# A one-core decoder layer: the first FFN's opening in a written order, reversed operand buffers, residual rows loaded a step ahead, and 32-column products in larger groups

## The chip, the cores and the metric

The kernel runs on one core of a Trainium2 chip. The core has five engines with a queue of instructions each: PE (TensorE, matrix products; its weight loads are listed apart as PEld), DVE (VectorE), ACT (ScalarE), POOL (GpSimd) and SP (SyncE, which here mainly issues DMAs). They run side by side and wait for each other through semaphores. The metric is the device time of one execution in microseconds (us), the median of the runs.

## The reference

One layer on 1024 tokens of width 1024, with 16 learned meta tokens in front. D_FF is 2816.

```python
h = concat([zeros(pad), meta, x])
h = h + 0.5 * swiglu(rms_norm(h, ffn1_norm), ffn1_w_in, ffn1_w_out)
u = rms_norm(h, mix_norm) @ w_in
...
o = concat([hgrn2(hq, hf, hi, hg, ...), stick_breaking(sq, sk, sv, ...)])
h = h + o @ w_out
h = h + 0.5 * swiglu(rms_norm(h, ffn2_norm), ffn2_w_in, ffn2_w_out)
return h[:, pad + N_META:, :]

def swiglu(h, w_in, w_out):
    g, u = split(h @ w_in, 2)
    return (silu(g) * u) @ w_out
```

The change touches the first FFN, and the first projection behind it by one weight tile.

## The kernel before

**Products.** All inputs are float32. A product of two float32 matrices is made of three matmuls on rounded parts: a number is cast to a high part (`hi`, `wh`) and its remainder (`lo`, `wl`) is kept, and hi·hi, lo·hi and hi·lo are added up in PSUM. The cast is ACT's, the remainder is DVE's. `halve` (L306) does it for the activations, `operand` (L356) for a weight block.

**Halves.** The FFN's two matrix products are block products of 2 by 2 halves that use seven half-size products in place of eight (Strassen's scheme in Winograd's form). For `fast_in` (L348, activations times `w_in`) the right operands are called B11, B21, T2, T3, T1, T4 and B22: B11, B21 and B22 are quarters of the normed, transposed tokens (512 features by 512 tokens each), the T's are sums and differences of them. The left operands are quarters of a weight column block (a11, a21, a22, a12) and sums of them (`s1`, `s2` and others), which POOL makes from loaded `raw` tiles (`made`, L382). One product of this kind, "a group" below, is `times` (L424): 12 matmuls of 128x128 by 128x512.

**A quad.** `quad` (L434) is a generator that makes one pair of column blocks: seven groups in turn, their weights taken one by one from `weights`. Results are added up over PSUM banks "qa", "qb", "qc" and kept copies (`p1`, `u2`, `u3`), and pass through `gate` (L498: SiLU on ACT) or `up` (L507: product on DVE), and the activations go to DRAM by DMAs that POOL issues (L514). `pair` joins the gate's quad and the up quad of the same columns.

**The opening.** PE can start before all operands exist: four pairs (eight quads) are opened by their first two groups, B11 and B21, 16 groups in all; then come the second groups by T2, and so on. Before the first group, `open_tokens` (L708) loads the first four 128-token rows, norms them (`norm_rows`, L679: sum of squares on ACT or DVE in turns, root on ACT, reciprocal and scale on DVE), turns them by 32 PE transposes (`turned`, L698) and makes B11's and B21's hi (L741) and lo (L744). The second four rows and the meta tokens follow while the opener groups run: b22 (L758), the combinations for T2 and T3 (L762, L763), the meta columns (L768), the T2 difference (L777) and its halves, and, spread over the steps, the halves of T3, T1, T4 (after a difference, L783) and B22. `setup_rest` (L101) makes constants for later stages: among them seven mask levels, each a memset on DVE (L114), four affine selects on POOL (L119, L123) and a copy on DVE (L127), all in one buffer `sd`, and two sigmoids on ACT (L135, L136). A scheduler orders the instructions of each engine by priorities; the program hands `fast_in` a `taken` hook that notes the last instruction of an engine in `marks`, and `issue_after` keeps an instruction behind a noted one.

**Residual rows.** `turn_x` (L827) is a generator with a step for each half of a 128-token row: load `xrow` (one buffer) by SP, four transposes (L837), a copy, a DMA to DRAM. `between` takes two steps after each opened pair.

**The second half.** `fast_out` (L569) multiplies the activations by `w_out` in the same scheme: `raw` blocks in a ring of six buffers (L587), seven steps (A11, S1, ..., A12, S3, A22), 11 q steps in each, 12 matmuls a q (L656). The meta tokens are 32 columns wide (`actm`): `meta` (near L1686) puts their small matmuls (`meta_block`, L1676 to L1678) between the q steps.

**The projection behind it.** A pool of weight tiles "we" holds two column tiles of `w_in` loaded during the FFN (`early_w`: key, value, query) for `project_early`; `sb_project` (L1114) loads column 2048 again in its first pass (L1131, as hi and lo halves, through `col_tile`, L237).

Of the kernel before, what the change touches and what calls it, by code (L numbers as in the profile page):

```python
# [20 lines left out]
P = 128  # L21
D = 1024
# [18 lines left out]
class Block:  # L41
# [59 lines left out]
    def setup_rest(self):  # L101
# [33 lines left out]
        nc.scalar.activation(self.lb, mx, AF.Sigmoid)  # L135
        nc.scalar.activation(self.lbc, mx, AF.Sigmoid, scale=-1.0)  # L136
# [211 lines left out]
    def fast_in(self, ops, n, w_in, actD, openers, ev0, open_ev, feed=None, meta=None, spare=None,  # L348
# [84 lines left out]
        def quad(col, take, opened=None, turns=0, keep=None):  # L433
# [3 lines left out]
            def go(bank, op, start):  # L437
                if start:
                    ps[bank] = pin.tile([P, n], F32, tag="q" + bank, name="q" + bank, bufs=2)
                left = ready.pop() if ready else next(w)  # L440
                if op not in made_yet:
                    next(feed)
                    made_yet.add(op)
                times(ps[bank], left, ops[op], start)
                return ps[bank]

            def first():
# [4 lines left out]
                nc.scalar.copy(p1, p)  # L452
                return p1

            def kept(name, x, y):
# [113 lines left out]
    def fast_out(self, hT, cs, n, w_out, actD, ready, between=lambda a, q: None,  # L569
# [37 lines left out]
        def left(step, q):  # L607
# [71 lines left out]
    def norm_rows(self, rows, at, junk):  # L679

        nc = self.nc
        for i, (row, m) in enumerate(rows, at):
            s, r = self.ss[:m, i, 0:1], self.ss[:m, i, 1:2]
            if i % 2:
                nc.vector.scalar_tensor_tensor(
                    junk[1][:m], row[:m], 1.0, row[:m], ALU.mult, ALU.mult, accum_out=s
                )
            else:
                nc.scalar.activation(junk[0][:m], row[:m], AF.Square, accum_out=s)
            self.root = nc.scalar.activation(  # L690
                r, s, AF.Sqrt, bias=self.eps[:m], scale=1.0 / D
            )
            nc.vector.reciprocal(r, r)
            nc.vector.tensor_scalar_mul(row[:m], row[:m], r)

    def turned(self, rows, ks, banks):
# [4 lines left out]
        for i, (row, _) in enumerate(rows):  # L701
# [6 lines left out]
    def open_tokens(self, ops, steps, rows_at, pool, operands):  # L708
# [7 lines left out]
        junk = [rp.tile([P, D], (BF16, U8)[i], name=f"junk{i}") for i in range(2)]  # L716

        def rows_in(r0):
            got = []
            for i in range(4):  # L720
                row = rp.tile([P, D], F32, tag="row", name="row", bufs=8)
                nc.sync.dma_start(row, x[r0 + i * P : r0 + i * P + P])
                got.append((row, P))
# [6 lines left out]
        rows = rows_in(0)  # L730
        kept = {}

        def spare(k):
            nc.scalar.mul((b11 + b21)[k], kept[k], g[k])

        with self.tc.high_priority():
            self.norm_rows(rows, 0, junk)
            kept.update(self.turned(rows, range(KT), "aabbccdd"))
            for k in range(KT):
                hi, lo = (t[:, k % 4, :] for t in ops[("B11", "B21")[k // 4]])  # L740
                nc.scalar.mul(hi, kept[k], g[k])  # L741
                if k == 0:
                    spare(0)
                stt(lo, kept[k], g[k], hi.bitcast(F32), ALU.mult, ALU.subtract)  # L744
        with self.tc.issue_after(self.root.ins):
# [21 lines left out]
        for k in range(KT):  # L767
# [3 lines left out]
        nc.vector.tensor_mul(  # L771
            self.xm[:, :, :META], ps, self.g1.unsqueeze(2).broadcast_to([P, KT, META])
        )
        rows_at.close()
        operands()
        for j in range(4):
            sub(t2[j], b22[j], b11[j])  # L777
            self.halve(ops["T2"], t2[j], j)
        next(steps)
        for o, b in (("T3", t3), ("T1", b11), ("T4", b21), ("B22", b22)):  # L780
# [4 lines left out]
            next(steps)  # L785

    def meta_in(self):
# [7 lines left out]
        def finish():  # L795
# [3 lines left out]
            if col < D_FF:  # L799
                nc.scalar.activation(self.sgm, ps, AF.Silu)  # L800
            else:
                f = (col - D_FF) // P
                nc.vector.tensor_mul(self.actm[:, f : f + 2, :META], ps, self.sgm)  # L803

        def begin(col, blocks):
# [16 lines left out]
            nc.scalar.copy(t, ps)  # L822
# [1250 lines left out]
```

## Time and profile before

| | |
|---|---|
| runs shown | 2073.99, 2076.32, 2076.86 us; median 2076.32 |
| profiled execution | 2080.41 us, its span 2078.7 us |
| granted TensorE clock over the span | 0.989 |
| busy share of the span | PE 96%, PEld 80%, DVE 65%, ACT 42%, POOL 32% |
| costliest group of matmuls | `qb<-T,wh` of `times`, 348.4 us |

The span is the profiled execution from its first to its last instruction. A row of the timeline gives the start and the length in us, the engine, the line, the operation, what it writes and reads, and how many instructions were put together; in brackets stands how long the engine had been idle before and which instruction released it. Lines like `PE xt L837 <- DMA xrow<-in_x_dram: 11.6, 4, 3.1` come from the view of waits: the total, the number of waits and the longest. In the chain of waits, each row is a piece of the path that ended last. Line numbers are those of the kernel before.

### The profile page before, as it was taken

The numbers are of one execution on the slowest core, as the hardware profiler recorded it, in microseconds if no ns is written. First come the engines' busy times: TensorE is split into PE (matmuls) and PEld (weight loads), VectorE is DVE, ScalarE is ACT, GpSimd is POOL, SyncE is SP. The second block draws the span as 40 slices with busy tenths as digits, with TensorE's granted clock in tenths as the row PEclk, the third lists the DMA queues.
The fourth block names the chain that finished last, engine by engine and source line by source line (L and its number), as shares of the span: only waits on it lengthen the run. The fifth ranks groups of instructions, "written<-read, shape, count | busy, mean of one in ns | idle before, by whom it ended". The sixth has DMA issues, their size and how long they took to land.

```text
span 2078.7 us, 30891 instructions
## 1 busy us (share of the span) xinstructions
PE 1998.4 (96%) x11004; PEld 1663.2 (80%) x11004; DVE 1344.6 (65%) x1984; ACT 867.8 (42%) x1760; POOL 675.4 (32%) x768
## 2 busy tenths in 40 slices
PE   6889999999999999999999999989999999999998
PEld 5777788777688777888889887878788888888887
DVE  6564467877586674225777667647577676777774
ACT  7322334333344443446667653535133233234443
POOL 3265455665100000223333323221164454440000
PEclk9999999999999999999999999999999999999999
DMA  4344488764895533643444428674633333359463
GB/s 149 101 143 147 149 257 262 248 207 172 280 314 163 171 116 105 180 147 120 135 136 128 128 68 275 160 216 179 211 118 102 101 102 101 109 206 332 129 198 137
DMA packets 283386, 348.23 MB, mean 168 GB/s; under 512 B 28049, under 2 KB 183185, under 8 KB 283233
## 3 DMA queue, kind: packets, MB, share of 16 engines
q1 hardware_dynamic: 263664, 289.03, 43.7%
q0 software_dynamic: 18528, 57.23, 7.9%
q8 instruction: 87, 1.43, 0.3%
q14 instruction: 67, 0.54, 0.1%
q10 hardware_dynamic: 1040, 0.00, 0.0%
HBM read 234.80 MB, written 111.38 MB: 167 GB/s over the span
## 4 chain that ended last, share of the span: by engine, by line
PE 68%; DVE 3%; DMA 2%; ACT 1%; issue 1%; SPq 0%; POOL 0%; DVEq 0%; POOLq 0%
PE o L656 20%; PE qb L428 9%; PE qc L428 6%; PE qa L428 6%; PE proj L249 5%; PE proj L250 5%; PE proj L251 5%; PE flip L1217 2%; PE wo L249 1%; PE wo L250 1%; PE wo L251 1%; PE oacc L1287 1%; PE oacc L1289 1%; PE z L1353 1%; PE lvl L1013 1%; PE z L1354 1%
## 5 line engine op out<-in xcount | busy, mean ns | idle before, releaser
L428 PE MATMUL qb<-T,wh 128*128 128x512 f32 x1056 | 348.4, 394 | 7.2 <-DVE actm L803 4.4
L360 DVE TENSOR_TENSOR wl<-s,wh 128x512 fp32r<-128x512 f32 x160 | 194.0, 1213 | 83.9 <-ACT wh L358 82.8
L428 PEld LDWEIGHTS qb<-T,wh 128*128 128x128 f32 x1056 | 200.0, 189 | 54.9 <-issue 9.5
L428 PE MATMUL qa<-B,wh 128*128 128x512 f32 x696 | 234.2, 402 | 9.0 <-ACT wh L358 4.0
L656 PE MATMUL o<-t,w 128*128 128x512 f32 x924 | 221.9, 397 | 3.2 <-DVE t L602 2.1
L249 PE MATMUL proj<-xh,wh 128*128 128x512 f32 (+2 forms) x640 | 217.8, 340 | 3.5 <-DMA wh<-win 2.7
L250 PE MATMUL proj<-xh,wl 128*128 128x512 f32 (+2 forms) x640 | 211.2, 330 | 0.4 <-DMA wl<-win 0.4
L251 PE MATMUL proj<-xl,wh 128*128 128x512 f32 (+2 forms) x640 | 210.7, 329 | 0.8 <-DVE xl L1666 0.8
L656 PE MATMUL o<-parts 128*128 128x512 f32 x924 | 209.9, 390 | 0.0
L656 PEld LDWEIGHTS o<-t,w 128*128 128x128 f32 x924 | 172.1, 189 | 45.1 <-issue 5.2
L428 PE MATMUL qb<-T,wl 128*128 128x512 f32 x528 | 207.4, 393 | 0.4 <-DVE wl L360 0.4
L358 ACT CAST wh<-s 128x512 fp32r<-128x512 f32 x160 | 99.5, 622 | 248.2 <-PE qb L428 155.2
L656 PEld LDWEIGHTS o<-parts 128*128 128x128 f32 x924 | 173.5, 188 | 35.8
L428 PEld LDWEIGHTS qa<-B,wh 128*128 128x128 f32 x696 | 134.7, 194 | 38.6 <-ACT wh L358 4.4
L382 POOL TENSOR_TENSOR s<-raw 128x512 f32<-128x512 f32 x80 | 109.2, 1366 | 146.1 <-DMA raw<-in_ffn_w_in_dram 97.5
L428 PE MATMUL qa<-B,wl 128*128 128x512 f32 x348 | 139.3, 400 | 9.9 <-DVE wl L360 9.9
L249 PEld LDWEIGHTS proj<-xh,wh 128*128 128x128 f32 x640 | 121.5, 190 | 14.4 <-DMA wh<-win 2.9
L360 DVE TENSOR_TENSOR wl<-raw,wh 128x512 fp32r<-128x512 f32 x120 | 118.5, 990 | 19.5 <-ACT wh L358 19.4
L251 PEld LDWEIGHTS proj<-xl,wh 128*128 128x128 f32 x640 | 121.2, 189 | 12.2 <-DVE xl L1666 1.2
L250 PEld LDWEIGHTS proj<-xh,wl 128*128 128x128 f32 x640 | 121.4, 190 | 10.1 <-DMA wl<-win 0.9
L358 ACT CAST wh<-raw 128x512 fp32r<-128x512 f32 x120 | 74.0, 621 | 123.7 <-PE qc L428 85.5
L1369 POOL TENSOR_TENSOR sig<-sig,keep 128x144 f32<-128x144 f32 (+3 forms) x64 | 81.3, 1272 | 134.0 <-DVE keep L1363 82.5
(383 smaller groups left out, 4132.1 us busy)
## 6 DMA issues: line engine op xcount, KB each, us to landing
raw<-in_ffn_w_in_dram SPq DMA_DIRECT2D x176, 256.0 KB, 3.9
raw<-in_ffn_w_out_dram SPq DMA_DIRECT2D x132, 256.0 KB, 4.0
w2in<-both SPq DMA_DIRECT2D x28, 512.0 KB, 3.2
raw<-in_w_in_dram SPq DMA_DIRECT2D x25, 512.0 KB, 4.0
ks<-kD SPq DMA_DIRECT2D x32, 260.0 KB, 4.8
wout<-both SPq DMA_DIRECT2D x16, 512.0 KB, 4.7
wh<-w2in SPq DMA_DIRECT2D x27, 256.0 KB, 3.5
wl<-w2in SPq DMA_DIRECT2D x27, 256.0 KB, 3.2
```

The costliest lines, as they stand in the source:

```text
L249: nc.tensor.matmul(ps, wh[:, s], xs, start=k == 0, stop=False)
L250: nc.tensor.matmul(ps, wl[:, s], xs, start=False, stop=False)
L251: nc.tensor.matmul(ps, wh[:, s], xl[:, k, c0 : c0 + n], start=False, stop=k == nk - 1)
L358: nc.scalar.copy(hi, src)
L360: nc.vector.tensor_sub(lo, src, hi.bitcast(F32))
L382: taken(op(t, x, y), False)
L428: nc.tensor.matmul(ps, a[:, k, :], b[:, k, :], start=start and k == 0 and i == 0, stop=k == 3 and i == 2, skip_group_check=True,)
L656: nc.tensor.matmul(banks[bank][m], y[:, m * P : (m + 1) * P], z, start=start and q == 0 and e == 0, stop=q == nq - 1 and e == 2, skip_grou ...
L1013: nc.tensor.matmul(ps[:, :, c, :], kp[:, P * c : P * c + P], strided(QA, P * c + n, (512 - n, 2), (2 * n, nb), (1, n)), start=True, stop=True,
L1217: self.nc.tensor.transpose(ps[:m, j, :], src[:, s0 : s0 + m], self.ident)
L1287: nc.tensor.matmul(o[:, c], vj, w[0], start=j == 0, stop=False, skip_group_check=True)
L1369: nc.gpsimd.tensor_mul(sig, sig, keep[:, 1 : nk + 1])
```

## The change

In the opening of the first FFN the order on ACT, DVE and SP is no longer left to the scheduler but is that of the program (`manual_schedule`). The sums, roots and scales of the rows are written apart, the first three rows' scales behind the third root. Each opener weight is made two groups ahead of its use. The transposes come in sets (features 0 to 5, then 6 and 7; the second rows' in two sets behind given groups). T2's halves lie beside the last four opener groups; the halves of T3, T1, T4 and B22 stand behind all of them, and `setup_rest` is put behind the marks. The buffers of the late operands are made in reversed order. `meta_in` holds its evictions behind the marks. `turn_x` loads a row right behind the transposes of the one before, and has one more step. In `fast_out`, S3's second block is loaded into the tile that held S2's operand (`s`) and not into the ring, and `meta` holds its blocks back: A12's and A22's products come at q = 2, 5, 8 and 10, S3's at its last q. The query's weight tile is kept from `project_early` to `sb_project`, and one pool of weight tiles, "wm", takes the place of two. The two sigmoids stand behind the FFN in the program.

```diff
...
-        nc.scalar.activation(self.lb, mx, AF.Sigmoid)
-        nc.scalar.activation(self.lbc, mx, AF.Sigmoid, scale=-1.0)
...
-                left = ready.pop() if ready else next(w)
+                left = ready.pop(0) if ready else next(w)
...
-                nc.scalar.copy(p1, p)
+                taken(nc.scalar.copy(p1, p), False)
...
-                nc.vector.tensor_add(t, y, x)
+                taken(nc.vector.tensor_add(t, y, x), False)
...
+                if not feed:
+                    for _ in range(2):
+                        ready.append(next(w))
+                        yield
...
-        for i in range(0, 2 * openers, 2):
-            for _ in range(2):
-                for q in opened[i : i + 2]:
-                    next(q)
-                    yield
         if feed:
+            for i in range(0, 2 * openers, 2):
+                for _ in range(2):
+                    for q in opened[i : i + 2]:
+                        next(q)
+                        yield
             next(opened[0])
             next(feed)
             made_yet.add("T2")
+        else:
+            yield opened
...
-                t = raw(1, 0, q)
                 if self.apart:
+                    nc.sync.dma_start(s, block(1, 0, q))
                     u = fresh()
-                    sub(u, a, t)
-                    return u, {(0, 0): a, (1, 0): t}
-                sub(a, a, t)
+                    sub(u, a, s)
+                    return u, {(0, 0): a, (1, 0): s}
+                sub(a, a, raw(1, 0, q))
...
+    def row_root(self, row, i):
+        m = row.shape[0]
+        s, r = self.ss[:m, i, 0:1], self.ss[:m, i, 1:2]
+        self.nc.scalar.activation(r, s, AF.Sqrt, bias=self.eps[:m], scale=1.0 / D)
+        self.nc.vector.reciprocal(r, r)
+    def row_scale(self, row, i, parts=1):
+        m = row.shape[0]
+        for j in range(parts):
+            t = row[:, D // parts * j : D // parts * (j + 1)]
+            self.nc.vector.tensor_scalar_mul(t, t, self.ss[:m, i, 1:2])
...
+        order = [q for i in range(0, len(opened), 2) for _ in range(2) for q in opened[i : i + 2]]
...
+        ra = rows_in(0)
+        for i in range(3):
+            self.row_sum(ra[i], i, junk, nc.vector if i == 1 else nc.scalar)
+            self.row_root(ra[i], i)
+        for i in range(3):
+            self.row_scale(ra[i], i)
+        self.row_sum(ra[3], 3, junk, nc.scalar)
+        self.row_root(ra[3], 3)
+        self.row_scale(ra[3], 3, 2)
+        next(order[0])
+        next(order[1])
+        rb = rows_in(512)
+        meta = rp.tile([META, D], F32, name="meta")
+        kept.update(self.turned(ra, range(6), "bbccdd"))
+        first(0, 1, 2, 3)
+        nc.vector.tensor_scalar_mul(b11[0], kept[0], g[0])
         spare(1)
-        next(steps)
-        rows = rows_in(512)
-        meta = rp.tile([META, D], F32, name="meta")
+        next(order[2])
         nc.sync.dma_start(meta, self.a["meta_tokens"])
-        for k in range(2, KT):
-            spare(k)
-        self.norm_rows(rows, 4, junk)
-        next(steps)
-        ps = self.turned(rows, range(4, KT), "bbcc")
-        for k in range(4, KT):
-            nc.scalar.mul(b22[k - 4], ps[k], g[k])
-        next(steps)
-        ps = self.turned(rows, range(4), "ddbb")
-        for j in range(4):
-            stt(b11[j], ps[j], g[j], b11[j], ALU.mult, ALU.subtract)
-            stt(t3[j], ps[j], self.ng1[:, j : j + 1], b22[j], ALU.mult, ALU.add)
-        self.norm_rows([(meta, META)], 8, junk)
-        next(steps)
-        ps = self.pin.tile([P, KT, META], F32, tag="qd", name="mps", bufs=2)
-        for k in range(KT):
-            nc.tensor.transpose(
-                ps[:, k, :], meta[:, k * P : (k + 1) * P], self.ident[:META, :META]
+        first(4, 5)
+        self.row_sum(rb[0], 4, junk, nc.vector)
+        next(order[0])
+        next(order[1])
+        kept.update(self.turned(ra, (6, 7), "bb"))
+        first(6, 7)
+        next(order[3])
...
+        def second(j):
+            if j == 0:
+                rows_at.close()
+                operands()
             sub(t2[j], b22[j], b11[j])
             self.halve(ops["T2"], t2[j], j)
-        next(steps)
-        for o, b in (("T3", t3), ("T1", b11), ("T4", b21), ("B22", b22)):
+        def roots():
+            for i, row in enumerate(rb + [meta]):
+                self.row_root(row, 4 + i)
+            for i in range(2):
+                self.row_scale(rb[i], 4 + i)
+        def scales():
+            for i in (2, 3):
+                self.row_scale(rb[i], 4 + i)
+            self.row_scale(meta, 8)
...
+        items = {
+            2: lambda: (spare(2, 3), sums(1)),
+            3: lambda: (spare(6, 7), sums(2)),
+            4: lambda: (self.row_sum(meta, 8, junk, nc.scalar), sums(3)),
+            5: roots,
+            6: lambda: (spare(4, 5), scales()),
+            7: keep_b22,
+            12: lambda: second(0), 13: lambda: second(1),
+            14: lambda: second(2), 15: lambda: second(3),
+        }
+        items.update({8 + j: lambda j=j: combine(j) for j in range(4)})
+        after = {6: turn_b22, 7: turn_b12, 8: turn_meta}
+        for i in range(2, len(order)):
+            if i + 2 < len(order):
+                next(order[i + 2])
+            items[i]()
+            next(order[i])
+            after.get(i, lambda: None)()
+        left = iter((("T3", t3), ("T1", b11), ("T4", b21), ("B22", b22)))
+        for o, b in left:
...
+    def meta_in(self, marks):
...
+            with ExitStack() as c:
+                for ins in marks.values():
+                    c.enter_context(self.tc.issue_after(ins))
+                if col < D_FF:
+                    nc.scalar.activation(self.sgm, ps, AF.Silu)
+                else:
+                    f = (col - D_FF) // P
...
-        for r0 in range(0, T, P):
-            m = min(P, T - r0)
-            for q in range(2):
-                row = pool.tile([P, 512], F32, tag="xrow", name="xrow", bufs=1)
-                self.load_rows(nc.sync, row, r0, m, slice(512 * q, 512 * q + 512))
-                ps = self.pin.tile([P, 4, P], F32, tag="qd", name="xt", bufs=2)
-                for k in range(4):
-                    nc.tensor.transpose(
-                        ps[:, k, :m], row[:m, k * P : (k + 1) * P], self.ident[:m, :m]
-                    )
-                t = pool.tile([P, 4, P], F32, tag="xt", name="xts", bufs=1)
-                nc.scalar.copy(t[:, :, :m], ps[:, :, :m])
-                nc.gpsimd.dma_start(
-                    xD[4 * q : 4 * q + 4, :, r0 : r0 + m].rearrange("k p t -> p k t"),
-                    t[:, :, :m],
+        places = [(r0, min(P, T - r0), q) for r0 in range(0, T, P) for q in range(2)]
+        def load(i):
+            r0, m, q = places[i]
+            row = pool.tile([P, 512], F32, tag="xrow", name="xrow", bufs=1)
+            self.load_rows(nc.sync, row, r0, m, slice(512 * q, 512 * q + 512))
+            return row
+        row = load(0)
+        yield
+        for i, (r0, m, q) in enumerate(places):
+            ps = self.pin.tile([P, 4, P], F32, tag="qd", name="xt", bufs=2)
+            for k in range(4):
+                nc.tensor.transpose(
+                    ps[:, k, :m], row[:m, k * P : (k + 1) * P], self.ident[:m, :m]
                 )
-                yield
+            t = pool.tile([P, 4, P], F32, tag="xt", name="xts", bufs=1)
+            nc.scalar.copy(t[:, :, :m], ps[:, :, :m])
+            nc.gpsimd.dma_start(
+                xD[4 * q : 4 * q + 4, :, r0 : r0 + m].rearrange("k p t -> p k t"),
+                t[:, :, :m],
+            )
+            if i + 1 < len(places):
+                row = load(i + 1)
+            yield
...
-            w = self.col_tile(self.a["w_in"][0], 2048)
+            w = self.early_w
...
-                        self.setup_rest()
+                        with ExitStack() as c4:
+                            for ins in marks.values():
+                                c4.enter_context(tc.issue_after(ins))
+                            self.setup_rest()
...
+                    opened = next(steps)
+                    with tc.manual_schedule(
+                        engines={nc.scalar.engine, nc.vector.engine, nc.sync.engine}
+                    ):
+                        self.open_tokens(
+                            ops, opened, rows_at, temps,
+                            lambda: operands(
+                                self.pool("t_ops", ctx=c2, side="right"),
+                                ("B22", "T4", "T1", "T3", "T2"),
...
+                    held = []
                     def meta(step, q, blocks):
-                        at = {"A12": [(0, 1, "x3")], "S3": [(0, 0, "y2"), (1, 0, "y3")],
-                              "A22": [(1, 1, None)]}.get(step, ())
-                        for i, j, bank in at:
-                            if q == 0 and bank:
-                                banks[i] = self.pout.tile([P, P], F32, tag=bank, name="m")
+                        banks_at = {"A12": {0: "x3"}, "S3": {0: "y2", 1: "y3"}, "A22": {}}
+                        if step not in banks_at:
+                            return
+                        held.extend((i, j, q, t) for (i, j), t in blocks.items())
+                        if q < last_q and (step == "S3" or q % 3 < 2):
+                            return
+                        for i, j, at, t in sorted(held, key=lambda x: x[0]):
+                            new = at == 0 and i in banks_at[step]
+                            if new:
+                                banks[i] = self.pout.tile(
+                                    [P, P], F32, tag=banks_at[step][i], name="m"
+                                )
                             meta_block(
-                                i, 2 * q + j, blocks[i, j], q == 0 and bool(bank),
-                                q == last_q and (i, j) != (1, 0),
+                                i, 2 * at + j, t, new, at == last_q and (i, j) != (1, 0)
                             )
+                        held.clear()
...
-                        if step == "A22" and q == 3:
+                        if step == "A22" and q == 5:
...
-                            self.weights("we", 2, 3, c2)
+                            self.weights("wm", 2, 3, c1)
...
+                    self.early_w = wq
...
-                self.weights("wm", 2, 2, c1)
                 pst = self.pool("st", ctx=c1)
+                nc.scalar.activation(self.lb, self.mx, AF.Sigmoid)
+                nc.scalar.activation(self.lbc, self.mx, AF.Sigmoid, scale=-1.0)
...
```

`marks` and `taken` are those of the kernel before, and `taken` now also notes `p1` and `u2`, `u3`; `ready` in `quad` is now taken from its front. `row_sum` is the square-and-add of `norm_rows` by itself, and `turn_b22`, `turn_b12`, `combine` and `turn_meta` are the old bodies of `open_tokens` under names.

More of the change, by code (lines that the diff above doesn't have):

```diff
@@ L677, in load_rows, with row_sum @@
             eng.dma_start(row[:m], x[r0 - META : r0 - META + m, cols])
[L679 to L686, printed above, removed]
-                )
[L688 to L691, printed above, removed]
-            )
-            nc.vector.reciprocal(r, r)
-            nc.vector.tensor_scalar_mul(row[:m], row[:m], r)
+    def row_sum(self, row, i, junk, eng):
+        nc, m = self.nc, row.shape[0]
+        s = self.ss[:m, i, 0:1]
+        if eng is nc.vector:
+            eng.scalar_tensor_tensor(
+                junk[1][:m], row, 1.0, row, ALU.mult, ALU.mult, accum_out=s
+            )
+        else:
+            nc.scalar.activation(junk[0][:m], row, AF.Square, accum_out=s)
+    def row_root(self, row, i):
[8 more added lines that the diff above has]
+            self.nc.vector.tensor_scalar_mul(t, t, self.ss[:m, i, 1:2])
     def turned(self, rows, ks, banks):
@@ L700, in turned @@
               for k, x in zip(ks, banks)}
-        for i, (row, _) in enumerate(rows):
+        for i, row in enumerate(rows):
             for k in ks:
@@ L722, in rows_in @@
                 nc.sync.dma_start(row, x[r0 + i * P : r0 + i * P + P])
-                got.append((row, P))
+                got.append(row)
             return got
@@ L729, in open_tokens, with spare @@
         b11, b21, b22, t2, t3 = (apart(x) for x in ("b11", "b21", "b22", "t2", "t3"))
-        rows = rows_in(0)
         kept = {}
[L733 to L738, printed above, removed]
-            for k in range(KT):
+        def spare(*ks):
+            for k in ks:
+                nc.scalar.mul((b11 + b21)[k], kept[k], g[k])
@@ new lines, in open_tokens, with turn_b22, keep_b22, turn_b12 @@
+        self.row_sum(rb[0], 4, junk, nc.vector)
[4 more added lines that the diff above has]
+        next(order[3])
+        def turn_b22():
+            kept["b22"] = self.turned(rb, range(4, KT), "bbcc")
+        def keep_b22():
+            for k in range(4, KT):
+                nc.scalar.mul(b22[k - 4], kept["b22"][k], g[k])
+        def turn_b12():
+            kept["b12"] = self.turned(rb, range(4), "ddbb")
+        def combine(j):
+            ps = kept["b12"][j]
+            stt(b11[j], ps, g[j], b11[j], ALU.mult, ALU.subtract)
+            stt(t3[j], ps, self.ng1[:, j : j + 1], b22[j], ALU.mult, ALU.add)
@@ new lines, in turn_meta @@
+        def turn_meta():
+            ps = self.pin.tile([P, KT, META], F32, tag="qd", name="mps", bufs=2)
+            for k in range(KT):
+                nc.tensor.transpose(
+                    ps[:, k, :], meta[:, k * P : (k + 1) * P], self.ident[:META, :META]
+                )
+            nc.vector.tensor_mul(
+                self.xm[:, :, :META], ps, self.g1.unsqueeze(2).broadcast_to([P, KT, META])
+            )
+        def second(j):
+            if j == 0:
+                rows_at.close()
+                operands()
```

45 lines of the change are left out of this document (16 added, 29 removed).

## The prediction

> **What bounds the kernel now.** I read the page first: shares, then the 40 slices, then what PE waits for, then the timeline of the stretches that the change touches.
>
> ```profile
> PE 1998.4 (96%) x11004; PEld 1663.2 (80%) x11004; DVE 1344.6 (65%) x1984; ACT 867.8 (42%) x1760; POOL 675.4 (32%) x768
> PE   6889999999999999999999999989999999999998
> PE xt L837 <- DMA xrow<-in_x_dram: 11.6, 4, 3.1
> ```
>
> PE is the bound: 96% of the span, and only the first slices (52 us each) are open. The third row is a group of PE's waits: 11.6 us in 4 waits on one line. So two things can pay: PE's idle time, and PE time itself. The opening, PE's rows alone:
>
> ```profile
> 8.98 6.48 PE L703 MATMUL xps<-ident,row 128*128 128x128 f32 x32 [8.98 <-DVE ss_x L693]
> 18.38 0.80 PE L428 MATMUL qa<-B,wh 128*128 128x512 f32 x1 [2.92 <-DVE B L744]
> 19.40 1.06 PE L428 MATMUL qa<-B,wh 128*128 128x512 f32 x2
> 20.68 1.03 PE L428 MATMUL qa<-B,wh 128*128 128x512 f32 x2
> 29.59 0.80 PE L428 MATMUL qa<-B,wh 128*128 128x512 f32 x1 [3.98 <-ACT wh L358]
> 39.81 1.91 PE L703 MATMUL xps<-ident,row 128*128 128x128 f32 x16
> 56.40 0.79 PE L428 MATMUL qa<-B,wl 128*128 128x512 f32 x1 [8.17 <-DVE wl L360]
> 69.22 0.50 PE L428 MATMUL qa<-B,wl 128*128 128x512 f32 x1 [1.52 <-DVE wl L360]
> 88.17 0.39 PE L428 MATMUL qb<-T,wh 128*128 128x512 f32 x1
> 517.68 2.72 PE qa L428 x12
> ```
>
> The brackets are idle time: four holes (2.92, 3.98, 8.17, 1.52), all behind casts and halves that ACT and DVE make too late. Three matmuls take 20.68 − 19.40 = 1.28 us behind the first hole, so 0.43 each, against 2.72 / 12 = 0.227 in full run: a hole is followed by slow matmuls. The 16 opener groups end at 88.17, where the first T2 group starts; the second starts one group later, at 90.9.
>
> **Part 1, the opening.** The hand-written order makes each opener weight two groups ahead and leaves the halves of T3, T1, T4 and B22, and `setup_rest` with its masks, until after the T2 halves. Rows for its steps:
>
> ```profile
> 9.90 0.17 DVE L693 RECIPROCAL ss_x<-ss_x 128x1 f32<-128x1 f32 x1 [0.21 <-ACT ss_x L690]
> 52.62 3.12 DVE L309 TENSOR_TENSOR T<-t,T 128x512 fp32r<-128x512 f32 x5
> 59.27 1.89 DVE L783 TENSOR_TENSOR b<-b,t 128x512 f32<-128x512 f32 x3
> 89.03 0.69 DVE L360 TENSOR_TENSOR wl<-s,wh 128x512 fp32r<-128x512 f32 x1
> 88.37 0.62 ACT L358 CAST wh<-s 128x512 fp32r<-128x512 f32 x1 [1.62 <-PE qa L428]
> 24.30 0.17 DVE L114 MEMSET sd<- 128x128 f32 x1
> 24.60 0.53 POOL L119 TENSOR_SCALAR_AFFINE_SELECT sd<-sd 128x64 f32<-128x64 f32 x2 [6.12 <-DVE sd L114]
> 25.09 0.54 POOL L123 TENSOR_SCALAR_AFFINE_SELECT sd<-sd 128x64 f32<-128x64 f32 x2
> 25.98 0.17 DVE L114 MEMSET sd<- 128x128 f32 x1
> 12.67 1.62 POOL L119 TENSOR_SCALAR_AFFINE_SELECT sd<-sd 128x64 f32<-128x64 f32 x2 [7.90 <-DVE ss_x L693]
> 14.25 1.10 POOL L123 TENSOR_SCALAR_AFFINE_SELECT sd<-sd 128x64 f32<-128x64 f32 x2
> 77.33 1.30 POOL L382 TENSOR_TENSOR s<-raw 128x512 f32<-128x512 f32 x1 [10.92 <-DMA raw<-in_ffn_w_in_dram]
> 78.72 1.62 POOL L382 TENSOR_TENSOR s<-s,raw 128x512 f32<-128x512 f32 x1
> ```
>
> Its PE time first. The first row's scale now waits for the third root: reciprocal done at 10.1, scale (0.7, as the other wide DVE work) at 10.8. From there 24 transposes at 6.48 / 32 (4.9) give 15.7, first matmul about 15.9. Then one slow group 12 × 0.43 = 5.1, eight transposes 1.1, fifteen groups at 2.72 = 40.8, two sets of sixteen transposes at 1.91 = 3.8, the meta transposes 0.7, and about 1 for the wait of the second rows' transposes on their scales: the openers end at E = 68.4 instead of 88.2, nearly 20 us earlier. Every weight is then at least one group ahead of its use, so I keep no hole.
>
> What is late next is the second T2 group. Its weight is a POOL result (two subtractions), cast on ACT, its low half on DVE. In the changed program's own order POOL has neg_b and all 28 affine selects in front of those two subtractions, each level waiting for a memset on DVE; and DVE has, between the last T2 half and this weight's low half, 16 other halves, four subtractions, the mask copies and memsets. In the old order this work stood inside the opener holes. Queued behind it: POOL's s, then ACT's cast, then PE's second T2 group and everything after. The ledger from E:
> - DVE: the last up product 0.66, eight halves of T3 and T1 at 3.12 / 5 = 0.62, one subtraction 1.89 / 3 = 0.63, small work 0.45: the first sd memset is done at E + 6.7.
> - A mask level costs 25.98 − 24.30 = 1.68 where DVE is free. Levels 0 to 2 have a T4 half and a subtraction beside them; I take 2.3 each: E + 13.6. Level 3 waits with its copy until T4's last and the four B22 halves are through (5 × 0.62 + 0.2), then u2's 0.66 and a memset: E + 17.7. Two more levels 3.4 and the last selects 1.5: POOL is free at E + 22.6.
> - POOL's s 1.30 + 1.62, ACT's cast 0.62: E + 26.1 = 94.5. PE waits 0.3 for the low half, and 12 slow matmuls cost 12 × 0.19 = 2.3 (the size that the query weight's hole shows below).
>
> PE had reached its second T2 group at 90.9 before; now it stands there at 94.5 + 0.3 + 2.3 = 97.1. So **the opening is +6.2**, although its sixteen groups end 20 us earlier. Bounds: with levels at 1.68 throughout and no slowing by neighbours, E + 24.2 gives +4; with a level's selects at 1.62 + 1.10 (the rows at 12.67 and 14.25, beside busy DVE) E + 32.8 and E one us late give +14. I sit nearer the first, because DVE has idle gaps from level 4 on. If the cover were not needed at all, the opening would be −20 (first rival).
>
> The Trainium skill speaks against the change here: its page "SBUF — State Buffer", section "🔬 SBUF: two separate sides", says that VectorE and GpSimd share a port pair as an exclusive lock, so that a VectorE operation with two SBUF inputs and a GpSimd operation that reads SBUF shut each other out. The pair of selects at 1.62 beside busy DVE against 0.53 beside idle DVE agrees. By that rule alone the halves beside levels 0 to 3 would come one after the other with the selects, an estimate of 3.4 us more, and the total would be 2069.4 instead.
>
> **Part 2, residual rows.** turn_x now loads row i + 1 right behind row i's transposes.
>
> ```profile
> 121.71 0.63 PE L837 MATMUL xt<-ident,xrow 128*128 128x128 f32 x4 [3.11 <-DMA xrow<-in_x_dram]
> ```
>
> The four waits come where two steps are taken back to back, the second step's row being loaded only then (one buffer). In the new order the first pair is split, since the first row is loaded by a yield of its own; pairs two to four are still back to back, and their second row is still asked for only behind the first's transposes. So −3.1 and not −11.6 (bounds 0 and −11.6).
>
> **Part 3, the 32-column products.** They come in visits of 8 matmuls between two quarter-steps of fast_out.
>
> ```profile
> 574.67 122.63 PE o L656 x540
> 697.23 0.43 PE L1678 MATMUL m<-ak,actm 128*32 128x128 f32 x8
> 700.79 0.43 PE L1678 MATMUL m<-ak,actm 128*32 128x128 f32 x8
> 739.69 0.43 PE L1678 MATMUL m<-raw,actm 128*32 128x128 f32 x8
> 743.00 0.43 PE L1678 MATMUL m<-raw,actm 128*32 128x128 f32 x8
> ```
>
> A q step without them takes 122.63 × 12 / 540 = 2.725. With one set of 8 (A12, A22) it is 743.00 − 739.69 = 3.31, with two sets (S3) 700.79 − 697.23 = 3.56. So a visit costs 0.335 once and each set 0.25. The sets stay; visits fall from 11 to 4 in A12 and in A22 and from 11 to 1 in S3, 24 in all: **−8.0**. If the whole excess went with the sets, 0; if a visit's whole 0.585 went, −14. The rest of this part (the S3 block reloaded into a tile that had its last reader, one add moved two steps) lies beside PE's 2.7 us steps; three raw tiles are now held for a group, see the second rival.
>
> **Part 4, the kept query weight.**
>
> ```profile
> 807.67 0.79 PE L249 MATMUL proj<-xh,wh 128*128 128x512 f32 x1 [2.70 <-DMA wh<-win]
> 808.88 0.80 PE L250 MATMUL proj<-xh,wl 128*128 128x512 f32 x1 [0.41 <-DMA wl<-win]
> 810.52 0.43 PE proj L250
> 820.63 0.24 PE proj L250
> ```
>
> Nothing has to land now: 2.70 + 0.41 go, and 12 matmuls at 0.43 instead of 0.24 (the last two rows, from the chain of waits), 2.3: **−5.4**. Bounds: −3.1 if the clock is slow anyway, 0 if the next column's load takes the wait over. The two sigmoids stand among the T4 casts on ACT, which is idle by then (their table load included); no path, 0.
>
> **Sum.** 6.2 − 3.1 − 8.0 − 5.4 = −10.3. The profiled execution took 2080.41 (span 2078.7 and 1.7 around it): 2070.1. The median of the runs shown is 2076.32, 4.1 lower; the same step from it gives **2066**.
>
> **The rivals.**
> R1, the second T2 weight is not held: the selects pass POOL quickly, or lie before E. For it: POOL was idle 6.12 before the level at 24.60. Against: the order on POOL is fixed and its first memset follows eight halves on DVE. Then −19.8 − 16.5 = −36: 2040. Chance 0.10.
> R2, slower: the ring of six raw tiles starves in A12 and A22.
>
> ```profile
> raw<-in_ffn_w_out_dram SPq DMA_DIRECT2D x16, 256.0 KB, 4.9
> DMA to landing us min/median/max: 2.9/4.9/5.9
> ```
>
> Three tiles held till their group's products leave three: 3 × 2.725 = 8.2 less cast and low half 1.3, so 6.9 for a refill, against 4.9 (at most 5.9) in fast_out's busiest stretch, 520 to 580. It decides beyond 6.9; six refills at 10 cost 6 × 3.1 = 18.6: 2085. The 1 us of margin speaks against it; that the new order leaves more loads queued at once speaks for it. Chance 0.12.
> R3, the cost of small products goes with the products, not the visits: part 3 is 0 and the total 2074, no change to be told. For it: two pitches fix two unknowns, with no third to test them. Chance 0.12.
> The rest (0.08): a mix beyond these, either side.
>
> **How the numbers follow.** Forecast 0.58. Its own range is from part 1's bounds (+4 to +14) with part 2 at its full −11.6 on the fast side: 2056 to 2074. The range for 8 in 10 takes R3 in and leaves out R1 and most of R2: 2056 to 2078. A measurement of this kernel tells 0.2% (4.2 us) from no change: faster means below 2072.2, slower above 2080.5. Faster: 0.53 of the forecast's 0.58, R1's 0.10, some of R3 and the rest, 0.70. Slower: R2 and a part of the rest, 0.14. Same: 0.16.
>
> **What would show it.** In the new profile: transposes from 10.8, no hole before 68, the first T2 group at 67 to 70, then one hole of 20 to 30 us on PE, ended by ACT's cast of s, with 28 selects on POOL inside it; three row waits left at the xt transposes; S3's q pitch 2.73 until one run of 176 small matmuls; no DMA wait near 805. Wrong would be: a T2 hole under 15 us (R1), waits on raw in A12 or A22 (R2), a group of small products that costs 0.585 a set (R3), or holes among the openers.

## The result and the profile after

| | before | after |
|---|---|---|
| median | 2076.86 us (5 runs, 2073.99 to 2080.98) | 2067.22 us (5 runs, 2065.67 to 2067.67) |
| profiled span | 2078.7 | 2065.3 |

The ratio is 0.995 with a 95% interval of 0.9936 to 0.9965: about 10 us less. The profiled executions differ by 13.4 us, more than the medians; where the other 3 to 4 us lie is shown below. From the page after:

```profile
PE 1982.5 (96%) x11004; PEld 1659.6 (80%) x11004; DVE 1361.4 (66%) x1988; ACT 867.7 (42%) x1758; POOL 672.8 (33%) x768
PE   7598999999999999999999998999999999999998
PE qb L426 <- ACT wh L356: 24.7, 1, 24.7
PE xt L918 <- DMA xrow<-in_x_dram: 8.9, 3, 3.5
```

The first slice is fuller than before (7 for 6), the second emptier (5 for 8): several holes became one. The last two rows, from PE's waits, name it, and show three row waits for four. The timeline of PE around the opening:

```profile
11.09 4.54 PE L712 MATMUL xps<-ident,row 128*128 128x128 f32 x24 [11.09 <-DVE pick L1618]
15.86 0.50 PE L426 MATMUL qa<-B,wh 128*128 128x512 f32 x1 [0.23 <-ACT B L755]
66.47 0.39 PE L426 MATMUL qb<-T,wh 128*128 128x512 f32 x1
94.08 0.79 PE L426 MATMUL qb<-T,wh 128*128 128x512 f32 x1 [24.73 <-ACT wh L356]
95.21 0.80 PE L426 MATMUL qb<-T,wl 128*128 128x512 f32 x1 [0.33 <-DVE wl L358]
```

No hole among the 16 opener groups: the first T2 group starts at 66.5 where it had started at 88.2. Then PE stands still for 24.73 us. What POOL, DVE, ACT and SP did meanwhile (some of their rows; in between lie more selects, halves and mask copies):

```profile
70.65 2.48 DVE L307 TENSOR_TENSOR T<-b,T 128x512 fp32r<-128x512 f32 x4
75.83 0.37 SPq L369 DMA_DIRECT2D raw<-in_ffn_w_in_dram  x1
77.56 1.47 POOL L119 TENSOR_SCALAR_AFFINE_SELECT sd<-sd 128x64 f32<-128x64 f32 x2 [0.67 <-DVE mx L134]
83.34 2.64 DVE L307 TENSOR_TENSOR B<-b,B 128x512 fp32r<-128x512 f32 x4
90.38 0.43 POOL L123 TENSOR_SCALAR_AFFINE_SELECT sd<-sd 128x64 f32<-128x64 f32 x2
90.78 1.26 POOL L380 TENSOR_TENSOR s<-raw 128x512 f32<-128x512 f32 x1
92.12 1.26 POOL L380 TENSOR_TENSOR s<-s,raw 128x512 f32<-128x512 f32 x1
93.41 1.84 ACT L356 CAST wh<-s 128x512 fp32r<-128x512 f32 x3 [9.15 <-POOL s L380]
94.06 3.37 DVE L358 TENSOR_TENSOR wl<-s,wh 128x512 fp32r<-128x512 f32 x3 [1.94 <-ACT wh L356]
```

The chain is read backwards: PE by ACT's cast at 93.4, that by POOL's two subtractions at 90.8 and 92.1, those by the last select, which ends at 90.8. The first raw block of this weight was asked for at 75.83 (SP's row) and had long landed.

To see where time is won or lost, one marker that both kernels have is followed: the small matmul `mf<-pick`, which stands between groups all through the first FFN. Before, then after:

```profile
103.00 0.30 PE L798 MATMUL mf<-pick,mt 128*128 128x32 f32 x2
239.24 0.30 PE L798 MATMUL mf<-pick,mt 128*128 128x32 f32 x2
497.16 0.30 PE L798 MATMUL mf<-pick,mt 128*128 128x32 f32 x2
504.89 0.47 PE L428 MATMUL qb<-T,wh 128*128 128x512 f32 x1 [3.46 <-DVE actm L803]
522.96 0.30 PE L798 MATMUL mf<-pick,mt 128*128 128x32 f32 x2
```

```profile
109.48 0.30 PE L867 MATMUL mf<-pick,mt 128*128 128x32 f32 x2
242.70 0.30 PE L867 MATMUL mf<-pick,mt 128*128 128x32 f32 x2
500.56 0.30 PE L867 MATMUL mf<-pick,mt 128*128 128x32 f32 x2
506.52 0.47 PE L426 MATMUL qb<-T,wh 128*128 128x512 f32 x1 [1.68 <-DVE actm L875]
522.96 0.30 PE L867 MATMUL mf<-pick,mt 128*128 128x32 f32 x2
```

After minus before: +6.48 behind the opening, +3.46 behind the four opened pairs (so −3.02 for the rows), +3.40 near 500, and 0 at 522.96. Between the last two stands a wait of PE that was 3.46 in the one and 1.68 in the other, with slow matmuls behind the longer. Whether that is the change's doing is taken up below.

The second half, from the chain of waits, before and then after:

```profile
771.38 0.36 PE m L1678 x8
771.74 0.43 PE proj L249
```

```profile
547.32 0.79 PE m L1768 x24
556.51 0.79 PE m L1768 x24
722.62 4.94 PE m L1768 x176
763.29 0.43 PE proj L247
```

Three q steps with one visit of 24 small matmuls take 556.51 − 547.32 = 9.19, that is 3 × 2.725 and 1.02 for the visit; a visit of 8 had cost 0.585 each time. The 176 of S3 take 4.94, or 0.22 for a set of 8. Both FFN stages stand level at 522.96, so the projection's start, 763.29 against 771.74, gives −8.45 for the second half, where the small products are. Behind the projection, the first attention product:

```profile
L1289 PE MATMUL oacc<-wu,v x160: 218/281/331, 975.3 to 1239.4; 128*64 128x256 f32 x128, 128*64 128x128 f32 x32
```

```profile
L1372 PE MATMUL oacc<-wu,v x160: 218/280/333, 961.7 to 1225.6; 128*64 128x256 f32 x128, 128*64 128x128 f32 x32
```

961.7 − 975.3 = −13.6, so −5.1 from the query weight; the rest of the kernel moves by no more than 0.2.

### The profile page after: what moved, and what is told of

The parts are those of the page before. It is cut to its first block, busy times and chain, and to the rows that moved or that the text cites. A ratio compares the mean times of both kernels' runs of the same rounds, so it can differ in the third digit from the quotient of the medians.

```text
span 2065.3 us, 30888 instructions
## 1 busy us (share of the span) xinstructions
PE 1982.5 (96%) x11004; PEld 1659.6 (80%) x11004; DVE 1361.4 (66%) x1988; ACT 867.7 (42%) x1758; POOL 672.8 (33%) x768
## 4 chain that ended last, share of the span: by engine, by line
PE 68%; DVE 4%; DMA 2%; ACT 1%; issue 1%; SPq 0%; DVEq 0%
PE o L660 18%; PE qb L426 9%; PE qc L426 6%; PE qa L426 6%; PE proj L247 5%; PE proj L249 5%; PE proj L248 5%; PE flip L1300 2%; PE wo L248 1%; PE wo L247 1%; PE wo L249 1%; DMA raw<-in_ffn_w_out_dram 1%; PE lvl L1096 1%; PE oacc L1370 1%; PE oacc L1372 1%
## 5 line engine op out<-in xcount | busy, mean ns | idle before, releaser
L358 DVE TENSOR_TENSOR wl<-s,wh 128x512 fp32r<-128x512 f32 x160 | 209.5, 1310 | 80.9 <-ACT wh L356 79.4
L426 PE MATMUL qa<-B,wh 128*128 128x512 f32 x696 | 229.7, 394 | 0.6 <-ACT B L755 0.2
L660 PE MATMUL o<-t,w 128*128 128x512 f32 x924 | 215.9, 394 | 2.8 <-DVE t L606 1.8
L426 PE MATMUL qa<-B,wl 128*128 128x512 f32 x348 | 136.0, 391 | 0.0
```

Of the source, the lines that this page charges most:

```text
L358: nc.vector.tensor_sub(lo, src, hi.bitcast(F32))
L426: nc.tensor.matmul(ps, a[:, k, :], b[:, k, :], start=start and k == 0 and i == 0, stop=k == 3 and i == 2, skip_group_check=True,)
L660: nc.tensor.matmul(banks[bank][m], y[:, m * P : (m + 1) * P], z, start=start and q == 0 and e == 0, stop=q == nq - 1 and e == 2, skip_grou ...
```

## The experiments

Three groups of runs, each with its own runs of the kernel before beside it. "Ratio" is against that, with its 95% interval; it is not the quotient of the two medians shown, so the two can differ by a few us.

**The kernel before once more, and the change's parts alone.** The first run has no edit.

> The kernel before, unchanged. Theory: its executions differ by more than those of the changed kernel (2073.99 to 2080.98 against 2065.67 to 2067.67), and a part of the 13.4 us between the two profiled spans is that: a median of 2075 to 2079. In the trace, the 3.46 us in which PE waited for DVE's actm near 505, behind one DVE instruction of 7.76 us, would be absent or of another size; the four row waits (11.6), the holes of the opening (2.92, 3.98, 8.17, 1.52) and the query weight's wait (2.70) would be there again. Rival: all of these sizes repeat to 0.2 us, and then the whole difference is the change's.

2076.85 us (ratio 1.001, 0.9991 to 1.0029), from 2071.08 to 2083.81. Its profiled span was 2073.1, 5.6 us below the one shown before. PE's waits and the timeline:

```profile
PE xt L837 <- DMA xrow<-in_x_dram: 11.4, 4, 3.1
PE qa L428 <- DVE wl L360: 9.9, 3, 8.2
502.03 0.47 PE L428 MATMUL qb<-T,wh 128*128 128x512 f32 x1 [1.08 <-DVE actm L803]
```

The holes and row waits repeat; the wait for actm does not (1.08 for 3.46). Over the thirteen traces of this document it is 2.26 to 3.71 in five, each time behind one DVE instruction of 6.56 to 7.89 us, and 1.08 to 1.69 in the other eight; both sizes come with the old opening and with the new one. So this wait differs between executions, and the surplus of 3.4 us in the pair of traces need not be the change's.

> The kernel before with the 32-column products in groups and S3's block in the operand's tile, nothing else. Theory: 24 visits fewer at 0.335 and 44 sets a little cheaper, so 8 to 9 us less than before, 2068 to 2069, all of it between the first A12 visit and the projection. Rival (cost goes with the products): 2076, as before. Second rival (three held raw tiles starve the ring): PE waits on w or raw in A12 and A22 and less than 5 us is gained.

```diff
-                        for i, j, bank in at:
...
+                        held.extend((i, j, q, t) for (i, j), t in blocks.items())
+                        if q < last_q and (step == "S3" or q % 3 < 2):
+                            return
```

2067.85 against 2076.09, −8.2 (ratio 0.9973, 0.9958 to 0.9988, which is 5.6 less, from 2.5 to 8.7). No wait on raw tiles appears in A12 or A22. The visits carry the cost, as predicted; the ring does not starve.

> The kernel before with the query's weight tile kept, nothing else. Theory: the waits of 2.70 and 0.41 near 805 and twelve slow matmuls (2.3) go: about 5 less than before, 2071 to 2072. Rival: the next column's load is late in its place, and the time stays within 1.5 us of before.

```diff
-            w = self.col_tile(self.a["w_in"][0], 2048)
+            w = self.early_w
```

2071.85 against 2076.09, −4.2 (ratio 0.9981, 0.9966 to 0.9997). The waits for `wh<-win` and `wl<-win` are gone and none takes their place.

> The kernel before with the opening's new order alone (row loads, small products and query weight as before). Theory: the sixteen opener groups end near 66 but the second T2 group starts near 94 behind the selects and halves, 6.5 us late at 124; the four row waits come as before: 4 to 7 us more than before, 2081 to 2084, slower. Rival: the end of the first FFN stands at one time whatever comes before it (both profiles have the same matmul at 522.96), and the total is that of before, 2076 to 2078.

The edit is the change without its rows, small products and query weight. 2079.05 against 2076.09, +3.0 (ratio 1.0021, 1.0006 to 1.0035). In its trace:

```profile
PE qb L426 <- ACT wh L356: 24.8, 1, 24.8
PE xt L912 <- DMA xrow<-in_x_dram: 11.5, 4, 3.1
```

So the hand-written opening alone makes the kernel slower, by a little less than the 4 to 7 us expected if the medians are taken, and by 4.4 if the ratio is. The marker is 5.9 late behind the opening (108.88 against 103.00) and 1.9 late at the end of the stage (524.87 against 522.96); between lies the wait for actm that varies, 1.69 here and 3.46 there. The parts sum to 3.0 − 8.2 − 4.2 − 3.0 (rows, from the traces) = −12.4, against −9.6 measured for the whole; each measured part has an interval of about 3 us either way, so the two agree no closer than that.

**What ends the hole, and the row waits.** These four start from the changed kernel.

> The changed kernel with setup_rest (memsets, 28 selects, mask copies) put behind the third opened pair, nothing else. Theory (the second T2 weight stood behind the selects on POOL): the hole after 69 stays, but ends near 84 and not at 94, since DVE still has 16 halves, four subtractions and u2 in front of the low half (68.3 to about 83) and the blocks of that weight are loaded only at 75.8: about 10 us less than the changed kernel, 2057. Rival (the hole is set by the halves and loads alone, selects cover nothing of it): still 94, 2067. Second rival: the selects stop DVE later, among the opened pairs, and give back over 5 us there.

```diff
                     def open_ev():
-                            self.setup_rest()
...
+                        if len(calls) == 5:
+                                self.setup_rest()
```

2066.69 us (ratio 0.9959): no gain over the changed kernel's 0.995. But the trace shows both halves of the expectation:

```profile
81.29 5.70 DVE L307 TENSOR_TENSOR B<-b,B 128x512 fp32r<-128x512 f32 x4
85.47 0.80 PE L426 MATMUL qb<-T,wh 128*128 128x512 f32 x1 [15.85 <-ACT wh L356]
88.72 0.79 PE L426 MATMUL qb<-T,wl 128*128 128x512 f32 x1 [2.45 <-DVE wl L358]
198.84 0.23 DVE L127 CAST masks<-sd 128x128 uint8<-128x128 f32 x1 [2.95 <-POOL sd L123]
202.40 0.76 PE L426 MATMUL qb<-T,wh 128*128 128x512 f32 x1 [4.76 <-DVE u L458]
```

The hole falls from 24.73 + 0.33 to 15.85 + 2.45 and the marker of 109.48 comes at 103.51, 6.0 us sooner. The selects held the second T2 weight, as predicted. What is left of the hole has two ends. POOL's first subtraction starts at 81.44, when the third block of this weight, asked for near 77, has landed; and the low half, 2.45 behind the cast, stands behind DVE's halves. Then the masks are paid among the opened pairs: DVE stands at a mask copy for POOL, PE for DVE's u, and in the fourth pair the marker (207.50) is back where the changed kernel had it (207.32). The second rival was right about the total.

> The changed kernel with one row step, not two, behind opened pairs two to four, nothing else. Theory (a row step waits only where two are back to back): no row wait is left, 8.9 us and the slow matmuls behind some of them (0 to 1.6 each) go: 9 to 13 us less, 2054 to 2058. Rival (the rows come late by the load queue, not by their order): the waits move to the single steps and less than 3 us is gained, 2064 to 2067.

```diff
+                        if len(calls) in (4, 6, 8):
+                            return
                         next(turning[0], None)
```

2054.24 us (ratio 0.9901, 0.9883 to 0.992): 13 below the changed kernel's first runs and 9.6 below its later ones (2063.84, in the next group). No row wait is left: the wait belongs to steps taken back to back.

> Both edits of the two runs before together. Theory: the gains add up, about 20 us less than the changed kernel, 2045 to 2049. Rival (later stages take it back): over 2052.

2057.05 us (ratio 0.9911, 0.9895 to 0.9927): not the sum. The opening's marker comes at 102.71, but PE waits 6.10 for DVE's actm at 201.99, among the masks. The rival holds.

> As the run before, with T4's subtractions and halves ahead of T3's, so that the blocks of the second T2 weight can be loaded about 5 us sooner. Theory (with the selects gone DVE's queue of halves ends the hole, not the loads): the cast of that weight may come sooner but its low half stands behind the same halves: within 2 us of the run before. Rival (the loads end the hole): 4 to 5 us less.

2059.01 us (ratio 0.9917, 0.9899 to 0.9935), within 2 us of the run before, as the theory had it. But the edit brought only half of the loads forward. SP asked for two of the four blocks at 70.86, 5 us sooner, and for the other two later than before, behind T3's halves:

```profile
78.56 0.92 SPq L369 DMA_DIRECT2D raw<-in_ffn_w_in_dram  x2
```

POOL's first subtraction takes the third block, which landed 2.8 us after that; it started at 81.54, where it had started at 81.13. The hole was 17.29 + 0.34 for 15.81 + 2.45: its cast came later and its low half sooner. So this run does not test the rival, and in both runs the cast's end of the hole goes back to a load.

**A better place for the masks and for the halves.**

> The changed kernel, unchanged. Theory: its terms repeat: hole of 24 to 25 us ended by ACT's cast, three row waits of 2.7 to 3.5, and a median of 2066 to 2068. Rival: the medians of 2067 for this kernel and for the one with later masks were by chance, and it moves by over 3 us.

2063.84 against 2077.32 (ratio 0.993, 0.9912 to 0.9948), from 2059.15 to 2065.3: 3.4 us below the first runs, outside what was expected and in the rival's range, while the intervals of the two ratios overlap. So differences of 3 us between medians of different groups of runs say little. Its hole is 24.47 + 0.34 and the three row waits 2.73, 3.52 and 2.78, so the terms repeat; but its four opened pairs took 130.2 from marker to marker where the first trace has 133.2.

> The run with the rows spread, and setup_rest in fast_out (A11, behind q 2), where POOL has little to do. Theory (the later masks gave back what the hole had won because DVE waited for selects among the opened pairs): the hole ends near 85, 15 to 18 us, nothing is given back, and the time is 6 us below the run with the rows spread: 2048. Rival (the selects cost PE the same wherever they stand): 2053 to 2055.

```diff
+                        if (step, q) == ("A11", 2):
+                            with tc.issue_after(self.last_w.ins):
+                                self.setup_rest()
```

2050.89 us (ratio 0.9871, 0.985 to 0.9891), 3 below the run with the rows spread, where 6 was expected; the intervals overlap, so the gain is not shown by the times. The marker stands at 103.38 (110.03 with only the rows spread), and in A11 and the step behind it PE waits 0.89, 0.71, 1.10 and 2.39 for `w`, 5.1 together, where the run with only the rows spread has one wait of 0.17. By the traces the masks cost less here, but not nothing.

> As the run before, and the halves of T3 and T1 and T4's differences moved from behind the opener groups to between groups 9 and 16, where DVE had 8.5 us idle from 35 to 69; B22's halves stay behind. Theory (the rest of the hole is DVE's queue and the loads that wait for T4's differences): the opener groups still end near 67, the blocks of the second T2 weight are asked for near 68, and the hole ends near 76: 7 to 9 us long, 2038 to 2042. Rival (opener weights are held up instead): holes among the openers from 50 to 67 of together over 5 us, 2044 or more.

```diff
+            12: lambda: halves("T3", t3, range(4)),
+            13: lambda: halves("T1", b11, range(4)),
+            14: lambda: (fourth(0), fourth(1)),
+            15: lambda: (fourth(2), fourth(3)),
```

2049.94 us (ratio 0.9872, 0.9851 to 0.9894): not told apart from the run before.

```profile
63.98 0.77 PE L426 MATMUL qa<-B,wh 128*128 128x512 f32 x1 [5.60 <-DVE sum L509]
82.89 0.79 PE L426 MATMUL qb<-T,wh 128*128 128x512 f32 x1 [5.80 <-ACT wh L356]
78.29 6.12 DVE L307 TENSOR_TENSOR B<-b,B 128x512 fp32r<-128x512 f32 x4
```

The hole shrank to 5.80 + 2.45, but 5.60 of it came back as a hole among the openers: DVE is busy for 13.6 of the 15 us from 55 to 70. The rival holds. The whole gain at the marker is 2.5 us (100.92 for 103.38).

## Why the prediction was right

Forecast 2066, measured 2067.22, the move −10.3 against −9.6. The mechanisms came as forecast; that the total came this close is in part luck, as the terms show:

- Opening, +6.2 forecast. The transposes started at 11.1 (10.8), the openers ended at 66.5 (68.4), the hole was ended by ACT's cast of s at 94.08 (94.5), with the 28 selects inside it; the marker says +6.48. Two errors nearly cancel. The openers were put 1.9 too late: the first group, taken for slow at 5.1, ran from 15.86 to 19.07, that is 3.2. And from the openers' end the ledger to the end of the cast was 1.5 too short, 26.1 for 27.6: the first three mask levels, held at 2.3 each, took 8.8 together (73.92 to 82.71 between their memsets on DVE) for 6.9. The first rival (no hole) falls. That POOL's selects were in front of that weight, and DVE's halves in front of its low half, is shown by the run with later masks: 6.0 us of it are the selects, and moving them only moved the cost.
- Rows, −3.1: the traces give −3.02, three waits of four left. The run with the rows spread takes away all three and shows that the order was the cause. That the sizes agree to 0.1 is luck. From marker to marker the four pairs with the old row loads took 136.2 and 136.0 in the two traces of the kernel before, 136.1 with only the opening changed, and 131.7 and 132.0 with only the groups or only the query weight; with the new loads they took 133.2 and 130.2. The averages differ by 2.7.
- Small products, −8.0: −8.45 in the trace, −8.2 alone by the medians. The second trace of the kernel before is 1.7 shorter from the same marker to the projection (518.44 to 765.5), so the traces give 6.7 to 8.5. The cost per visit was right (0.34 from the new pitch: 1.02 − 3 × 0.22); the sets, held at 0.25, also became cheaper. The third rival falls. The second falls as well: no wait on raw.
- Query weight, −5.4: −5.1 in the trace, −4.2 alone. Nothing took the wait over.

What the sum did not have is the 3.4 us near 505. The wait is in the trace of before that was used and not in its repeat, so it was right to leave it out of the forecast, and wrong to expect the next pair of traces to differ by the sum alone.

The early selects took up to 1.47 a pair beside busy DVE against 0.43 at the end. Of the 3.4 us more that were estimated by the Trainium skill's rule on the shared ports ("SBUF — State Buffer", section "🔬 SBUF: two separate sides"), the 1.9 of the first three mask levels are seen. The total does not show them, because the openers ended 1.9 sooner than forecast.

## What to carry to other kernels

Work that one engine does for later hides in another engine's holes; when the holes are closed, look up where that work goes in each engine's order, and price it there. A hand-written order covers only the engines named in it: here POOL is not among them, and the 28 selects that stood in its order ahead of a weight were what PE came to wait for. When a stall goes after one move and the total stays, follow one marker through both traces; it tells which stage took the time back.

## What was not expected

A DVE instruction that reads two SBUF tiles can take many times its usual length beside busy POOL. In the kernel before, DVE and POOL near 500:

```profile
496.39 7.76 DVE L360 TENSOR_TENSOR wl<-raw,wh 128x512 fp32r<-128x512 f32 x1
496.83 1.28 POOL L527 TENSOR_TENSOR t<-sg,t 128x512 f32<-128x512 f32 x1
498.06 1.29 POOL L199 TENSOR_TENSOR sum<-early,sum 128x512 f32<-128x512 f32 x1
499.85 1.30 POOL L382 TENSOR_TENSOR s<-raw,s 128x512 f32<-128x512 f32 x1
501.10 1.27 POOL L199 TENSOR_TENSOR sum<-early 128x512 f32<-128x512 f32 x1
502.33 1.25 POOL L382 TENSOR_TENSOR s<-raw 128x512 f32<-128x512 f32 x1
```

7.76 us for what takes 0.69 elsewhere, while POOL goes from one instruction to the next (with a DMA issue of 0.55 at 499.29); PE's 3.46 us for actm stand behind it. The four B22 halves did the same beside POOL's s: 5.70 and 6.12 where four take 2.48. The Trainium skill ("SBUF — State Buffer", section "🔬 SBUF: two separate sides") describes one port pair that either engine locks for a whole instruction, whichever starts first. These rows agree that one engine stands still while the other works, and not that the first keeps the pair: DVE's instruction starts at 496.39, ahead of POOL's at 496.83, and ends behind five of POOL's. Why DVE comes last so many times in a row is not shown by any run here.

Whether the slow clock follows a wait of about 3 us is not the same each time. The granted clock in four stretches of the kernel before, one for each row wait (by columns: stretch, length, busy time of PE, PEld, DVE, ACT and POOL with counts, then the clock, the DMA share and GB/s):

```profile
118.00:134.00 16.00, 12.89 (x84) 10.76 (x86) 7.40 (x13) 4.37 (x8) 9.93 (x11) 1.00 0.40 149
152.00:168.00 16.00, 13.33 (x92) 10.98 (x90) 8.41 (x12) 4.19 (x7) 9.95 (x11) 1.00 0.38 145
185.00:205.00 20.00, 16.93 (x95) 13.70 (x94) 7.08 (x13) 4.33 (x8) 9.87 (x11) 0.83 0.47 158
222.00:240.00 18.00, 15.29 (x83) 12.57 (x86) 5.42 (x8) 5.03 (x9) 9.98 (x11) 0.91 0.32 117
```

Waits of 3.11 and 2.67 left it at 1.00, waits of 3.08 and 2.71 brought it to 0.83 and 0.91. What decides it stays open.
